# Weights split ahead and kept in DRAM, skewed bias rows, and shifted steps in one branch of a hybrid attention block

## The chip, the cores and the metric

The kernel runs on one core of one Trainium2 chip. The metric is the device time of one execution in microseconds (us), the median of several runs. The core has five engines that run in parallel, each through its own queue in order: TensorE (PE, with its weight loads as PEld), VectorE (DVE), ScalarE (ACT), GpSimd (POOL) and SyncE (SP). SP issues all DMA transfers here.

## The reference

One layer of a streaming encoder on 1024 tokens of width 1024, in float32. Two token mixers run beside each other: branch A is softmax attention over a band of 9 chunks of 64 tokens with a learned bias by clipped distance, branch B is stick-breaking attention, causal, without softmax. Each has 8 heads of 64 channels. Both are projected, gated by a sigmoid of two further projections of x, added, projected again, and a layer norm and a gated feed-forward part of width 2816 with a second layer norm follow.

```
h = x @ w_in[l]
qa, ka, va, qb, kb, vb, ga, gb = jnp.split(h, split_pts, axis=-1)
y_a = chunk_band_attention(heads_a(qa), heads_a(ka), heads_a(va), rel_bias[l]) @ w_proj_a[l]
y_b = stick_breaking_attention(heads_b(qb), heads_b(kb), heads_b(vb)) @ w_proj_b[l]
gate_a = jax.nn.sigmoid(ga + b_gate[l, :D])
gate_b = jax.nn.sigmoid(gb + b_gate[l, D:])
mix = (gate_a * y_a + gate_b * y_b) @ w_out[l]
x = layer_norm(DEEPNORM_ALPHA * x + mix, ln1_g[l], ln1_b[l])
g, u = jnp.split(x @ w_ffn_in[l], 2, axis=-1)
x = layer_norm(DEEPNORM_ALPHA * x + (jax.nn.silu(g) * u) @ w_ffn_out[l], ln2_g[l], ln2_b[l])
```

In branch A the bias of a query i and a key at position p of its band is `rel_bias[h, clip(512 + i - p, -256, 256) + 256]`, so the bias row of each query is that of the one before, moved by one place.

## The kernel before

**Numbers.** TensorE multiplies in a fast type with fewer bits, so each float32 operand is split into a high part (an ACT copy into that type) and a low part (a subtract of the high part, on DVE or POOL), and each product is three matmuls: high by high, high by low, low by high. `split` (line 108) and `begin_w` (line 430) do this. A weight tile is 128 x 1024.

**Stages.** (1) The start, and stage one to about 343 us: q, k, v of both branches and the first five pairs of gates, as 17 pairs of weight tiles. One pair is seven products of twelve matmuls over sums and differences of operands, run by `run_pairs` (line 410) over the steps of `pair_steps` (line 182). Each product ends in a PSUM bank which ACT copies or DVE adds out, and which a later product of the same pair goes on to fill. `left` and `right` load and split the weights of the next pairs while one runs, `also` is called after each pair, and q, k, v and the gates are stored to DRAM. (2) Attention, 343 to 661 us, described below. (3) Branch B's projection to 705 us, the output projection and first layer norm to 797 us, and the feed-forward part to the end.

**The order of attention** is written out by hand in the loop at line 821. It runs over 16 heads (8 of A, then 8 of B), each with 12 value steps: 8 for the first half of the queries (g 0) and 4 for the second (g 1). At a step the loop
- loads q, k and the bias of a head two ahead (`load_qk`, at step 8) and v of the next head (`load_v`, at step 4);
- issues score blocks up to the number in `LEAD` (line 37): eight of 128 queries for each head. `LEAD[0]` is A's, `LEAD[1]` B's; its entry at a step says how many blocks, counted from the head's first, have been issued by then, and more than 8 means blocks of the next head. A's block (`soft_block`) is a score product of two matmuls for each of one or two cuts into a bank `sc`, a DVE reduction that adds the bias and finds the extreme, an exponential on ACT, a reciprocal on DVE and a scaling on POOL. B's block (`stick_block`) has two sigmoids on ACT, a running product on DVE and a product on POOL;
- counts down the list `later` of delayed jobs and runs those that are due;
- transposes a block of the weights (`turn`: TensorE into `tp`, then a split by ACT and DVE into `pt`);
- issues filler matmuls (`fill_until`) and, once more than `LAG` = 2 are pending, the oldest value product (`mult`) into the single bank `pv`. The last product of a half is followed by an ACT copy of that bank into `yt` or `yv`, a small transfer and, three steps later, a POOL add.

**The fillers** (`fill_all`, line 695) are TensorE work that depends on no head: the remaining six gate products (`gate`, gates 10 to 15) and, when A's heads are done, A's projection (`yAps`). For each, `begin_gate` or `begin_proj` loads the weight's tile raw from the inputs, and half a product later ACT makes the high part and POOL the low one.

**The bias of a head** (`rel_bias_tile`, line 556). `small_inputs` (line 315) writes one row of 896 values for each head to DRAM, reversed by DVE. For a head, a transfer whose rows start one element apart brings 128 x 640 values to `braw`, ACT reverses and negates them into `bias`, and POOL sets two corners.

**`split_y`** (line 765) splits a finished output of two heads for the projections; for the last tiles it is put on `later`, two steps after the POOL add.

**Memory.** `SLOTS` names groups of 128 x 1024 tiles in SBUF; QKV is a ring of eight of them that stage one uses for its results. A tile's next use waits until its last use is done, whichever queue that is on.

Of the kernel before, what the change touches and what calls it, by code (L numbers as in the profile page):

```python
# [33 lines left out]


LAG = 2
LEAD = ((6, 7, 9, 9, 10, 10, 11, 11, 12, 12, 13, 13), (7, 8, 9, 9, 10, 10, 11, 11, 12, 12, 13, 14))

FILL = (18.0, 42.0)

# [7 lines left out]
def hybrid_trunk_kernel(ctx: ExitStack, tc, x, xt, w_in, b_gate, rel_bias, w_proj,  # L48
# [29 lines left out]
    def dram(name, n):  # L78
        return [dr.tile([P, 1024], F32, name=f"{name}{i}") for i in range(n)]
# [24 lines left out]
    ORDER = (1, 2, 6, 5, 7, 3, 4)  # L104
    s_dr = [[dram(f"s_dr{g}_{hf}_", 7) for hf in range(2)] for g in range(4)]
    rel_dr = dr.tile([8, 896], F32, name="rel_dr")

    def split(dst_h, dst_l, src):
        nc.scalar.copy(dst_h, src)  # L109
# [205 lines left out]
    def small_inputs():  # L315

        rel_sb = cycle(QKV, "rel_sb")[0:8, 0:896]
        rel_in = cycle(QKV, "rel_in")[0:8, 0:N_REL]
        dma(rel_in, rel_bias)
        nc.vector.tensor_copy(rel_sb[:, 383:896], rel_in[:, ::-1])  # L320
        nc.vector.tensor_copy(rel_sb[:, 0:383], rel_in[:, 512:513].to_broadcast([8, 383]))
        dma(rel_dr, rel_sb)
        dma(bg, b_gate)

    def store_hl(d, hi, lo):
# [30 lines left out]
    def project(i):  # L356
# [50 lines left out]

        return pair_steps(f"p{i}", Wa[i], ops_x, c, done, "pv" if i == 3 else "mm")

    def run_pairs(steps, left, right, also=lambda i: None, first=2, aside=lambda i: None,  # L410
                  then=lambda: None):

        n = len(steps)
        for j in range(first):
            steps[j][0]()
            steps[j][1]()
        then()
        for i in range(n):
            rest = steps[i][2:] if i < first else steps[i]
            for j, p in enumerate(rest):  # L420
                p()
                if j == 0 and i + 1 < n:
                    right(i + 1)
                if j == 1 and i + 2 < n:
                    left(i + 2)
                aside(i)
            also(i)
# [16 lines left out]
    def load_w(*args):  # L444
        return begin_w(*args)()

    def of(tag):
        return lambda name, dtype=F32: slot(tag, name, dtype)

    def begin_gate(i, lo_eng):  # L450
        return begin_w(w_in[24 + (i % 2) * 8 + i // 2], f"g{i}", of("op"), of("op"), lo_eng)

    def gate(i, w, half_way, freed=None):
# [49 lines left out]
    def rest_of_start():  # L503
# [3 lines left out]
        for kt in range(4):  # L507
# [2 lines left out]

    run_pairs([project(i) for i in range(1, len(work))],
              lambda i: left(i + 1) if i > 2 else left_again(3) if i == 2 else None,
              lambda i: right(i + 1), first=3, then=rest_of_start, also=lambda i: small_inputs() if i == 2 else None)
    first_gate = 2 * N_GATE
    first_w = begin_gate(first_gate, nc.vector)()


# [36 lines left out]
        return [t[0][:, 0:512], t[0][:, 512:896], t[1][:, 0:256], t[1][:, 256:384]]  # L554

    def rel_bias_tile(head):
        braw = slot("kp", f"braw{head}")
        src = rel_dr[head:head + 1, 0:640]
        dma(braw[:, 0:640],
            bass.AP(tensor=src.tensor, offset=src.offset, ap=[[1, P], [1, 640]]))  # L560
        bias = slot("kp", f"bias{head}")
        nc.scalar.activation(bias[:, 0:640], braw[:, 0:640][:, ::-1], AF.Copy, scale=-1.0)  # L562
        nc.gpsimd.memset(bias[0:DH, 576:640], BIG)  # L563
        nc.gpsimd.memset(bias[DH:P, 0:DH], BIG)
        return bias
# [66 lines left out]
    def value_steps(hd, g, wt):  # L632

        br, h = hd["br"], hd["h"]
        reach = (4, 8)[br]
        q0 = 4 * g
        nm = f"{'ab'[br]}{hd['n']}_{g}"
        pv = []

        kbs = [4, 5, 6, 7, 3, 2, 1, 0] if g == 0 else [7, 6, 5, 4]  # L640
        steps = []
        for i, kb in enumerate(kbs):
            lo_q = max(q0, kb - reach)
            hi_q = min(q0 + 3, kb)
            n = (hi_q - lo_q + 1) * P
            pts = []

            def turn(kb=kb, lo_q=lo_q, hi_q=hi_q, n=n, pts=pts):
                tp = bank("tr", f"tp_{nm}_{kb}")
                for qb in range(lo_q, hi_q + 1):  # L650
                    tr(tp[:, (qb - lo_q) * P:(qb - lo_q + 1) * P],  # L651
                       wt[qb - q0][:, (kb - qb) * P:(kb - qb + 1) * P], ident)
                pt = slot("pt", f"pt_{nm}_{kb}", F32R)
                split(pt[:, 0:n], pt[:, HW:HW + n], tp[:, 0:n])
                pts.append(pt)

            def mult(i=i, kb=kb, lo_q=lo_q, n=n, pts=pts):
                v = hd["v"]
                if i == 0:
                    pv.append(bank("pv", f"pv_{nm}"))  # L660
                last = i == len(kbs) - 1
                cs = slice((lo_q - q0) * P, (lo_q - q0) * P + n)
                pt = pts[0]
                mm(pv[0][:, cs], v[:, kb, :], pt[:, 0:n], start=(i == 0), stop=False)
                mm(pv[0][:, cs], v[:, kb, :], pt[:, HW:HW + n], start=False, stop=last)
                if last:
                    yt = hd["yt"]()
                    r = slice(h * DH, (h + 1) * DH)
                    gs = slice(g * HW, (g + 1) * HW)
                    if hd["i"] == 7:  # L670
                        nc.scalar.copy(yt[r, gs], pv[0][DH:P])
                        nc.vector.tensor_tensor(yt[r, gs], pv[0][0:DH], yt[r, gs], ALU.add)
                    else:

                        if g == 0:
                            hd["yv"] = slot("yt", f"yv_{nm}")
                        yv = hd["yv"]
                        both, other = (yt, yv) if h == 0 else (yv, yt)
                        nc.scalar.copy(both[:, gs], pv[0])
                        dma(other[r, gs], both[(DH, 0)[h]:(P, DH)[h], gs])  # L680

                        def add():
                            nc.gpsimd.tensor_tensor(yt[r, gs], yt[r, gs], yv[r, gs], ALU.add)
                            if h == 1 and g == 1:
                                if hd["i"] > 4:
                                    later.append([2, lambda: split_y(hd["i"], yt, nc.gpsimd)])
                                else:
                                    dma(y_dr[hd["i"]], yt)
                        later.append([3, add])

            steps.append((turn, mult))
        return steps


    def fill_all():
        w = first_w
        got = []
        for i in range(first_gate, 15):
            end = begin_gate(i + 1, nc.gpsimd)
            yield from gate(i, w, lambda: got.append(end()))  # L700
            w = got.pop()
        end = begin_proj(0, 0, "op", nc.gpsimd)
        ends = {}

        def freed(k):
            if k == 0:
                got.append(end())
            if k < 4:
                ends[k] = begin_y(k, nc.gpsimd)
            if k > 1:  # L710
                ends.pop(k - 2)()

        yield from gate(15, w, lambda: None, freed)
        w = got.pop()
        gates = {0: begin_gA(0)}
        for cc in range(4):
            if cc < 3:
                end = begin_proj(0, cc + 1, "op", nc.gpsimd)
            for j in range(2):
                c = 2 * cc + j  # L720
                t = gates.pop(c)
                squash(t, c, 0)
                if c < 7:
                    gates[c + 1] = begin_gA(c + 1)
                for hf, cs in enumerate((LO, HI)):
                    acc = bank("mm", f"yAps{c}_{hf}")
                    if j == 1 and hf == 0 and cc < 3:
                        got.append(end())
                    for k in range(4):
                        ks = slice(j * HW + k * P, j * HW + (k + 1) * P)  # L730
                        for n, (lw, rx) in enumerate(((w[0], yh), (w[0], yl), (w[1], yh))):
                            mm(acc, lw[:, ks], rx[k][:, cs], start=(k == n == 0),  # L732
                               stop=(k == 3 and n == 2))
                            yield 1.0
                    nc.vector.tensor_tensor(t[:, cs], acc, t[:, cs], ALU.mult)
                if c < KEEP:
                    dma(m_dr[c], t)
                else:
                    kept[c] = t
                if c == 0:  # L740
                    end_y = begin_y(4, nc.gpsimd)
                elif c == 1:
                    end_y()
            if cc < 3:
                w = got.pop()
# [75 lines left out]
    for si, (hd, g, st, box) in enumerate(vsteps):  # L821
# [18 lines left out]
        goal += FILL[hd["br"]] / nhead  # L840
        fill_until(0.5 * (last + goal))
        pend.append(mult)
        if len(pend) > LAG:
            pend.pop(0)()
        fill_until(goal)
    for m_ in pend:
# [391 lines left out]
```

## Time and profile before

| | us |
|---|---|
| median of 3 runs | 1454.58 |
| lowest and highest | 1454.35, 1455.19 |
| the profiled execution's own time | 1453.11 |
| its span in the trace | 1451.1 |

The granted TensorE clock was 0.998 of full speed. Where the trace is read below, rows give an engine, a line of the kernel, the operation, the tile written, an arrow and the tiles read, with a count or a time. `[0.54 <-DVE st_a L582]` says that the engine had been idle for 0.54 us, and that what ended the wait was DVE's instruction of that line. Rows of the table by stage give the stretch and its length, then busy time and instructions of PE, PEld, DVE, ACT and POOL, the granted clock, the share of the DMA engines and GB/s. Ends of matmuls are modelled, so a busy PE may still be waiting. Transfers are told by issue on SP's queue; in the list of transfers the last two figures are KB of one and us from issue to landing. One stall is counted once in each queue that shows it (PE and PEld), so the two are not added.

### The profile page before, as it was taken

The page shows a single profiled execution, that of the slowest core. Times are in us where ns is not written, and L with a number is a line of the kernel's source. Part 1 is how long each engine was busy: PE and PEld are TensorE (multiplying, and loading weights), DVE is VectorE, ACT ScalarE, POOL GpSimd, SP SyncE. Part 2 cuts the span into 40 slices and gives each one's busy share as a digit, 9 for nine tenths or more (in the row PEclk, how much of TensorE's full clock was granted, in tenths as well). Part 3 has the DMA queues.
Part 4 walks back from the last instruction along what each step waited for, and adds up shares of the span by engine and source line. Part 5 has one row for each costly group of instructions (what it writes and reads, how often), then busy time and mean ns, then how long its engine had stood idle before and what let it go on. Part 6 is the DMA issues. An engine that isn't in the chain of part 4 may idle for free.

```text
span 1451.1 us, 19140 instructions
## 1 busy us (share of the span) xinstructions
PE 1429.5 (99%) x6748; PEld 1181.2 (81%) x6748; DVE 1024.4 (71%) x1644; ACT 682.7 (47%) x1187; POOL 278.9 (19%) x326
## 2 busy tenths in 40 slices
PE   9999999999999999999999999999999999999997
PEld 7888888888888788877888888888888887888886
DVE  8875565434776878877849966676677755978767
ACT  6444444446878878874313633444444433221201
POOL 0000000003655879850014000000000000100016
PEclk9999999999999999999999999999999999999999
DMA  7555545338667477647502123344444457787602
GB/s 247 156 178 174 174 148 186 110 101 255 196 191 199 131 226 229 204 178 239 186 25 94 66 102 114 134 159 160 160 159 145 151 197 250 286 307 242 205 15 102
DMA packets 83167, 246.15 MB, mean 170 GB/s; under 512 B 10480, under 2 KB 10480, under 8 KB 83072
## 3 DMA queue, kind: packets, MB, share of 16 engines
q1 hardware_dynamic: 83072, 244.94, 50.8%
q8 instruction: 53, 0.87, 0.2%
q14 instruction: 42, 0.34, 0.1%
HBM read 161.51 MB, written 79.72 MB: 166 GB/s over the span
## 4 chain that ended last, share of the span: by engine, by line
PE 90%; DVE 4%; ACT 2%; issue 1%; DMA 1%; POOL 1%; SPq 0%; POOLq 0%; DVEq 0%; ACTq 0%
PE sxf L179 15%; PE sxp L179 12%; PE szf L179 7%; PE dx L1171 6%; PE szp L179 6%; PE syf L179 4%; PE gps L460 4%; PE syp L179 3%; PE dz L1171 3%; PE yAps L732 2%; PE tp_b L651 2%; PE ops L119 2%; PE ops L117 2%; PE ops L116 2%; PE fpswh_h L116 2%; PE fpswh_h L119 2%
## 5 line engine op out<-in xcount | busy, mean ns | idle before, releaser
L1127 POOL TENSOR_TENSOR wdyt<-wdyt 128x512 f32<-128x512 f32 x8 | 10.7, 1336 | 515.7 <-DVE wdgt L1126 485.1
L628 POOL TENSOR_TENSOR w_b<-w_b,kp_b 128x511 f32<-128x511 f32 (+3 forms) x96 | 97.4, 1029 | 26.9 <-DVE kp_b L623 16.9
L623 DVE TENSOR_TENSOR_SCAN kp_b<-kp_b,ident_ps 128x512 f32<-128x512 f32 (+2 forms) x64 | 56.5, 883 | 24.9 <-ACT kp_b L620 24.6
L891 POOL TENSOR_TENSOR mv<-mv,neghalf 128x1 f32<-128x1 f32 x16 | 23.9, 1491 | 210.9 <-DVE mv L890 210.9
L563 POOL MEMSET bias<- 64x64 f32 x8 | 1.2, 145 | 327.8 <-ACT bias L562 327.8
L192 DVE TENSOR_TENSOR c<-sxp,c 128x512 f32<-128x512 f32 x16 | 11.1, 691 | 69.8 <-issue 40.2
L620 ACT ACTIVATE kp_b<-sc_b 128x512 f32<-128x512 f32 (+3 forms) x96 | 48.4, 504 | 23.9 <-PE sc_b L546 22.9
L110 DVE TENSOR_TENSOR pt_b<-tp_b,pt_b 128x512 fp32r<-128x512 f32 (+1 forms) x96 | 50.3, 543 | 8.4 <-ACT pt_b L109 7.7
L179 PE MATMUL szf<-x1S63h,wcf 128*128 128x512 f32 x168 | 55.1, 389 | 0.0
L1102 DVE TENSOR_TENSOR x<-dx,x 128x512 f32<-128x512 f32 x64 | 43.2, 686 | 15.5 <-PE dx L1171 15.5
L110 DVE TENSOR_TENSOR sl<-h,sl 128x512 fp32r<-128x512 f32 x56 | 38.4, 685 | 19.4 <-ACT sl L109 19.4
L593 POOL TENSOR_SCALAR w_a<-w_a,st_a 128x640 f32<-128x640 f32 (+2 forms) x64 | 42.8, 671 | 48.2 <-DVE st_a L592 33.0
L110 DVE TENSOR_TENSOR pt_a<-tp_a,pt_a 128x512 fp32r<-128x512 f32 (+1 forms) x96 | 45.8, 486 | 8.1 <-ACT pt_a L109 6.9
L651 PE MATMUL tp_b<-ident,w_b 128*128 128x128 f32 x288 | 47.7, 274 | 3.7 <-DVE pt_b L110 3.4
L109 ACT CAST pt_b<-tp_b 128x512 fp32r<-128x512 f32 (+1 forms) x96 | 47.3, 499 | 8.2 <-PE tp_b L651 7.4
L109 ACT CAST sl<-h 128x512 fp32r<-128x512 f32 x56 | 34.7, 620 | 33.7 <-PE syf L179 17.1
L116 PE MATMUL ops<-wh_o,mh 128*128 128x512 f32 x128 | 50.2, 392 | 0.0
L119 PE MATMUL ops<-wh_o,ml 128*128 128x512 f32 x128 | 50.0, 391 | 0.0
L117 PE MATMUL ops<-wl_o,mh 128*128 128x512 f32 x128 | 49.9, 390 | 0.0
L621 ACT ACTIVATE w_b<-sc_b 128x511 f32<-128x511 f32 (+3 forms) x96 | 48.5, 506 | 0.0
L109 ACT CAST pt_a<-tp_a 128x512 fp32r<-128x512 f32 (+1 forms) x96 | 40.0, 426 | 18.2 <-PE tp_a L651 16.9
L588 ACT ACTIVATE w_a<-w_a,st_a 128x640 f32<-128x640 f32 (+2 forms) x64 | 44.7, 698 | 5.2 <-DVE st_a L582 4.3
(1890 smaller groups left out, 4807.2 us busy)
## 6 DMA issues: line engine op xcount, KB each, us to landing
s_dr<-sl SPq DMA_DIRECT2D x112, 256.0 KB, 2.3
sd<-s_dr SPq DMA_DIRECT2D x56, 512.0 KB, 4.5
wLf<-in_w_ffn_in_dram SPq DMA_DIRECT2D x22, 512.0 KB, 4.5
wRf<-in_w_ffn_in_dram SPq DMA_DIRECT2D x22, 512.0 KB, 3.6
wRp<-in_w_in_dram SPq DMA_DIRECT2D x17, 512.0 KB, 4.7
wLp<-in_w_in_dram SPq DMA_DIRECT2D x17, 512.0 KB, 5.4
v_dr<-v SPq DMA_DIRECT2D x16, 512.0 KB, 4.5
kl<-k_dr SPq DMA_DIRECT2D x32, 256.0 KB, 5.4
```

Of the source, the lines that this page charges most:

```text
L109: nc.scalar.copy(dst_h, src)
L110: nc.vector.tensor_tensor(dst_l, src, dst_h.bitcast(F32), ALU.subtract)
L116: mm(acc, lh, rh, start=(i == 0), stop=False)
L117: mm(acc, lh, rl, start=False, stop=False)
L119: mm(acc, ll, rh, start=False, stop=(i == n))
L179: mm(acc, lw[:, ks], rx, start=(first and kt == i == 0), stop=(kt == 3 and i == 2), skip_group_check=not first)
L460: mm(acc[hf], lw[:, ks], rx[k][:, (LO, HI)[hf]], start=(k == j == 0), stop=(k == KT - 1 and j == 2))
L621: nc.scalar.activation(be[:, m0:e], sc[:, m0 - c0:n], AF.Sigmoid)
L623: nc.vector.tensor_tensor_scan(kp[:, 0:e], kp[:, 0:e], ident_ps()[:, 0:e], 0.0, ALU.mult, ALU.add)
L628: nc.gpsimd.tensor_tensor(be[:, m0:e], be[:, m0:e], kp[:, m0 - 1:e - 1], ALU.mult)
L651: tr(tp[:, (qb - lo_q) * P:(qb - lo_q + 1) * P], wt[qb - q0][:, (kb - qb) * P:(kb - qb + 1) * P], ident)
L1171: mm(acc, a, b, start=(first and i == n == 0), stop=(i == n - 1 == 1), skip_group_check=not first)
```

## The change

1. **Weights split in stage one.** Nine weights that the fillers use (gates 11 to 15 and the four tiles of A's projection) are loaded after the pairs 7 to 15 of stage one's loop, split there (high part on ACT, low part on DVE) and stored as two tiles in DRAM. In attention `begin_split` loads the two tiles, and no ACT copy or POOL subtract is left for them.
2. **Bias by one transfer.** `small_inputs` negates on ACT and does not reverse; eight transfers inside DRAM write each head's row 128 times, each one element further right. A head's bias is then one transfer, without ACT.
3. **Steps of branch A.** `LEAD[0][1]` is 8 instead of 7, so A's last score block goes out at step 1 instead of step 2, and at step 2 of the second half of A's queries one value product less is taken out, so its first product comes a step later.
4. **`split_y`** of the last tiles is put six steps after the POOL add instead of two.

```diff
-LEAD = ((6, 7, 9, 9, 10, 10, 11, 11, 12, 12, 13, 13), ...
+LEAD = ((6, 8, 9, 9, 10, 10, 11, 11, 12, 12, 13, 13), ...
...
+    skew_dr = [dr.tile([P + 1, 1024], F32, name=f"skew_dr{h}") for h in range(8)]
...
-        nc.vector.tensor_copy(rel_sb[:, 383:896], rel_in[:, ::-1])
-        nc.vector.tensor_copy(rel_sb[:, 0:383], rel_in[:, 512:513].to_broadcast([8, 383]))
+        nc.scalar.activation(rel_sb[:, 0:513], rel_in, AF.Copy, scale=-1.0)
+        nc.scalar.activation(rel_sb[:, 513:896], rel_in[:, 512:513].to_broadcast([8, 383]),
+                             AF.Copy, scale=-1.0)
         dma(rel_dr, rel_sb)
+        for h in range(8):
+            src, dst = rel_dr[h:h + 1, 128:896], skew_dr[h][0:1, 128:896]
+            dma(bass.AP(tensor=dst.tensor, offset=dst.offset, ap=[[1025, P], [1, 768]]),
+                bass.AP(tensor=src.tensor, offset=src.offset, ap=[[0, P], [1, 768]]))
...
+    first_gate = 2 * N_GATE
+
+    def aside_work(i):
+        if i == 2:
+            small_inputs()
+        first = len(work) - 1 - len(ws_dr)
+        if i >= first:
+            store_split(i - first)
...
+    ws_dr = [dram(f"ws_dr{i}_", 2) for i in range(15 - 2 * N_GATE + 4)]
+
+    def store_split(i):
+        n = 15 - 2 * N_GATE
+        if i < n:
+            j = 2 * N_GATE + 1 + i
+            srcs = w_in[24 + (j % 2) * 8 + j // 2]
+        else:
+            srcs = [(cs, w_proj[2 * (i - n) + j][:, 0:HW]) for j, cs in enumerate((LO, HI))]
+        take = lambda name, dtype=F32: cycle(QKV, name, dtype)
+        for d, t in zip(ws_dr[i], load_w(srcs, f"pre{i}", take, take, nc.vector)):
+            dma(d, t.bitcast(F32))
+
+    def begin_split(i, name):
+        hl = [slot("op", f"w{p}_{name}", F32R) for p in "hl"]
+        for d, t in zip(ws_dr[i], hl):
+            dma(t.bitcast(F32), d)
+        return lambda: hl
...
     def begin_gate(i, lo_eng):
+        if i > first_gate:
+            return begin_split(i - first_gate - 1, f"g{i}")
         return begin_w(w_in[24 + (i % 2) * 8 + i // 2], f"g{i}", of("op"), of("op"), lo_eng)
...
-              lambda i: right(i + 1), first=3, then=rest_of_start, also=lambda i: small_inputs() if i == 2 else None)
-    first_gate = 2 * N_GATE
+              lambda i: right(i + 1), first=3, then=rest_of_start, also=aside_work)
...
     def rel_bias_tile(head):
-        braw = slot("kp", f"braw{head}")
-        src = rel_dr[head:head + 1, 0:640]
-        dma(braw[:, 0:640],
-            bass.AP(tensor=src.tensor, offset=src.offset, ap=[[1, P], [1, 640]]))
         bias = slot("kp", f"bias{head}")
-        nc.scalar.activation(bias[:, 0:640], braw[:, 0:640][:, ::-1], AF.Copy, scale=-1.0)
+        dma(bias[:, 0:640], skew_dr[head][0:P, 256:896])
...
-                                    later.append([2, lambda: split_y(hd["i"], yt, nc.gpsimd)])
+                                    later.append([6, lambda: split_y(hd["i"], yt, nc.gpsimd)])
...
-        end = begin_proj(0, 0, "op", nc.gpsimd)
+        end = begin_split(15 - first_gate, "y0_0")
...
-                end = begin_proj(0, cc + 1, "op", nc.gpsimd)
+                end = begin_split(16 - first_gate + cc, f"y0_{cc + 1}")
...
-        if len(pend) > LAG:
+        wait = hd["br"] == 0 and (g, st) == (1, LAG)
+        while len(pend) > LAG + wait:
             pend.pop(0)()
```

More of the change, by code (lines that the diff above doesn't have):

```diff
@@ L36 @@
 LAG = 2
-LEAD = ((6, 7, 9, 9, 10, 10, 11, 11, 12, 12, 13, 13), (7, 8, 9, 9, 10, 10, 11, 11, 12, 12, 13, 14))
+LEAD = ((6, 8, 9, 9, 10, 10, 11, 11, 12, 12, 13, 13), (7, 8, 9, 9, 10, 10, 11, 11, 12, 12, 13, 14))
 FILL = (18.0, 42.0)
```

## The prediction

> **What bounds the kernel now.** I read the page first, then a table of the engines' busy time by stage, then the lists of waits of TensorE's two queues, then the order of time around the longest waits.
>
> ```profile
> span 1451.1 us, 19140 instructions
> PE 1429.5 (99%) x6748; PEld 1181.2 (81%) x6748; DVE 1024.4 (71%) x1644; ACT 682.7 (47%) x1187; POOL 278.9 (19%) x326
> PE 90%; DVE 4%; ACT 2%; issue 1%; DMA 1%; POOL 1%; SPq 0%; POOLq 0%; DVEq 0%; ACTq 0%
> ```
>
> TensorE is busy for 99% of the span and carries 90% of the chain that ended last. The change adds and removes no matmul, so it can only win TensorE's gaps or make new ones. The table by stage (PE, PEld, DVE, ACT, POOL busy) says where the gaps are:
>
> ```profile
> 36.00:343.00 307.00, 306.87 (x1382) 252.99 (x1382) 174.63 (x235) 136.82 (x191) 2.99 (x5) 1.00 0.51 160
> 343.00:366.00 23.00, 22.48 (x130) 18.04 (x129) 17.35 (x70) 20.35 (x47) 11.78 (x18) 1.00 0.74 218
> 366.00:462.00 96.00, 92.76 (x576) 80.83 (x575) 73.49 (x266) 75.56 (x194) 54.90 (x75) 1.00 0.67 197
> 462.00:493.00 31.00, 29.21 (x160) 22.76 (x158) 25.12 (x44) 29.10 (x65) 24.21 (x37) 1.00 0.60 182
> 575.00:635.00 60.00, 56.47 (x310) 46.89 (x309) 49.33 (x70) 46.89 (x102) 48.78 (x62) 1.00 0.63 195
> ```
>
> Stage one (the projections, 36 to 343) leaves 307.00 - 306.87 = 0.13 us: nothing to win there, only to lose. The four stretches of attention leave 0.52, 3.24, 1.79 and 3.53 us, 9.1 in all. What PE and its weight queue PEld waited for (total us, times, longest), PE's two rows first:
>
> ```profile
> PE tp_b L651 <- DVE pt_b L110: 3.4, 5, 1.0
> PE sc_a L545 <- DVE st_a L582: 2.0, 6, 0.5
> ...
> PEld sc_a L545 <- DVE st_a L582: 4.7, 11, 0.7
> PEld pv_a L664 <- ACT yt L679: 2.5, 5, 0.8
> PEld tp_a L651 <- DVE pt_a L110: 1.8, 3, 1.0
> PEld tp_a L651 <- POOL w_a L593: 1.7, 5, 0.7
> PEld pv_a L664 <- ACT yv_a L679: 1.4, 3, 0.5
> ```
>
> The two queues differ because the ends of matmuls are modelled. One head boundary of branch A, in order of time, shows which is nearer, with a later undisturbed pair of transposes:
>
> ```profile
> 398.53 0.38 PE L651 MATMUL tp_a<-ident,w_a 128*128 128x128 f32 x2
> 398.61 0.56 ACT L679 COPY yt<-pv_a 128x512 f32<-128x512 f32 x1
> 399.19 0.40 ACT L588 ACTIVATE w_a<-w_a,st_a 128x128 f32<-128x128 f32 x1
> 399.21 0.19 PEld L545 LDWEIGHTS sc_a<-kh,qs 128*128 128x128 f32 x1 [0.54 <-DVE st_a L582]
> 399.84 0.40 PE L664 MATMUL pv_a<-pt_a,v 128*128 128x512 f32 x1
> ...
> 409.14 0.38 PE L651 MATMUL tp_a<-ident,w_a 128*128 128x128 f32 x2
> 409.28 0.47 PE L460 MATMUL gps<-xh,wh_g 128*128 128x512 f32 x1
> 409.90 0.19 PEld L664 LDWEIGHTS pv_a<-pt_a,v 128*128 128x128 f32 x1 [0.46 <-ACT yv_a L679]
> ```
>
> Two transposes and the next start are 409.28 - 409.14 = 0.14 us apart undisturbed, and 399.21 - 398.53 = 0.68 at the boundary: 0.54 lost, as PEld says. So I size steady stalls by PEld, as an upper bound, and take PE's rows as the lower.
>
> **The change, part by part.** The sum is made against the profiled execution: 1451.1 of span and 2.0 around it are 1453.1 us, 1.5 below the median of the three runs, 1454.58. I carry the difference over to that median.
>
> *Work taken from ACT and POOL in attention.* The rows of the removed operations:
>
> ```profile
> L439 ACT CAST wh_g<-wr_g x6: 1047/1048/1063, 328.2 to 447.1; 128x1024 fp32r<-128x1024 f32 x6
> L440 POOL TENSOR_TENSOR wl_g<-wr_g,wh_g x5: 2374/2404/2406, 337.8 to 470.2; 128x1024 fp32r<-128x1024 f32 x5
> L562 ACT ACTIVATE bias<-braw x8: 722/740/767, 320.9 to 415.9; 128x640 f32<-128x640 f32 x8
> L440 DVE TENSOR_TENSOR wl_g<-wr_g,wh_g x1: 1224/1224/1224, 329.4 to 329.4; 128x1024 fp32r<-128x1024 f32 x1
> ```
>
> Nine weights lose 9 x 1.05 = 9.4 us of ACT and 9 x 2.40 = 21.6 of POOL, and eight bias rows lose 8 x 0.74 = 5.9 of ACT. In their place SP loads two tiles of 512 KB for each weight instead of one; the second transfer comes where 1.05 + 2.40 us of splitting were, so the weight is ready no later. Busy time off the path is worth nothing; what counts is the wait behind which such an operation stands. At the start of branch A (343 to 366) ACT and POOL each ran one behind the other, and the first transposes waited 1.7 us (PEld) for POOL's normalised rows. One cast less ahead of the first exponentials starts them about 1 us earlier. I take 0.8 us won; bounds 0 and 1.7.
>
> *LEAD 7 to 8.* The last score block of each A head (128 wide) now goes out one step earlier, beside the block before it; with its two matmuls go DVE's reduction, ACT's exponential and POOL's scaling of that block, and no transfer. So DVE has read both score banks sooner when the next head's 320-wide halves want them. That removes the cause of sc_a <- st_a. It does not all come back. ACT's order becomes: the three last exponentials, the fifth pt cast, then the yt copy that frees the only pv bank. In the rows above the copy (398.61) stood ahead of the last exponential (399.19); behind it and the cast it would end near 400.05, and the first value product would start at about 400.07 instead of 399.84, 0.23 later. Of 0.54 at a boundary I leave about 0.3: 0.24 won, six times, 1.5 us. Bounds: 4.7 won (the whole PEld row), or 8 x 0.23 = 1.8 lost with no stall gone.
>
> *The extra lag.* At step (g 1, st 2) of branch A the first value product waits one step more, so the single pv bank's copy gets about one transpose and one gate matmul more: 0.07 by the pair above and 0.23 by stage one's steps (twelve matmuls of 512 columns in 2.72 us, below), 0.30 us against the 0.46 shown. Only two matmuls move, and nothing of SP's or POOL's. By the rows of yt and yv_a, 2.5 + 1.4 = 3.9 us over 8 waits; some of these are the boundary's first product. I take 2.2 won; bounds 0.7 (the share that PE's own gaps show, 0.15 in this instance) and 3.9.
>
> *A to B (462 to 493).* POOL no longer has the 2.4 us subtract ahead of the first stick-breaking products, but DVE's scans set most of the 1.8 us there. I take 0.5 won; bounds 0 and 1.8.
>
> *split_y six steps later, and no proj split in branch B.* In order of time, the two places where branch B lost most:
>
> ```profile
> 580.79 1.05 ACT L768 CAST yh<-yt 128x1024 fp32r<-128x1024 f32 x1 [0.49 <-POOL yt L683]
> 585.66 2.39 POOL L769 TENSOR_TENSOR yl<-yraw,yh 128x1024 fp32r<-128x1024 f32 x1
> 586.73 0.63 PE L651 MATMUL tp_b<-ident,w_b 128*128 128x128 f32 x4 [1.02 <-DVE pt_b L110]
> ...
> 627.05 1.05 ACT L768 CAST yh<-yt 128x1024 fp32r<-128x1024 f32 x1 [3.04 <-POOL yt L683]
> 628.17 2.40 POOL L769 TENSOR_TENSOR yl<-yt,yh 128x1024 fp32r<-128x1024 f32 x1 [1.00 <-ACT yh L768]
> 629.89 0.19 PEld L545 LDWEIGHTS sc_b<-kh,qs 128*128 128x128 f32 x1 [0.68 <-ACT w_b L621]
> 631.57 0.44 PE L651 MATMUL tp_b<-ident,w_b 128*128 128x128 f32 x2 [1.00 <-DVE pt_b L110]
> ```
>
> ACT stood 3.04 us in order behind a cast whose input POOL had not finished; queued behind it were the sigmoids of the next block, and behind those DVE's scan, POOL's product and the transposes. With the cast further back both should pass. I take 2.0 us of 1.02 + 0.68 + 1.00 = 2.7; bounds 0 (the cast and the 2.4 us subtract meet another crowded step) and 2.7.
>
> *What stage one pays.* Nine casts (1.05) go to ACT and nine subtracts (1.22) to DVE, one pair of them per pair of products, 19 us: on DVE 174.63 of 307 was busy, on ACT 136.82. SP gets 9 weights more to load and 18 stores. What such a cast stands in front of is a copy that frees a bank:
>
> ```profile
> 316.02 0.59 ACT L209 COPY c<-szp 128x512 f32<-128x512 f32 x1 [2.13 <-PE szp L179]
> L205 ACT COPY c<-sxp 128x512 f32<-128x512 f32 x16 | 9.4, 589 | 32.2 <-PE sxp L179 23.8 <-DMA q_dr<-c 4.6 <-DMA wLp<-in_w_in_dram 3.9
> DMA to landing us min/median/max: 4.1/5.1/5.9
> ```
>
> The last cast goes ahead of the copy at 316.02, where ACT idled 2.13 us: 1.08 us are left over. Copies come one step of twelve matmuls apart, 2.13 + 0.59 = 2.72 us; TensorE needs the bank one such step after the copy could begin, and the copy takes 0.59, so the cast may be another 2.1 us late, about 3.2 in all. The second row is the evidence that a late DMA in ACT's order is survived: 8.5 us of waits for DMAs, while PE lost 0.13. The third row is the landing of the gate weights: a spread of 1.8 us, inside 3.2. I take 0.7 us lost in all. Bounds: 0, and where the spread meets only the 1.08 us, 9 x (1.8 - 1.08) = 6.5 lost.
>
> [...]
>
> *The skewed bias rows.* Eight transfers inside DRAM, 128 rows of 3 KB each, are issued after the store of the relative bias, where SP's next issue was late anyway:
>
> ```profile
> 98.40 0.94 SPq L130 DMA_DIRECT2D wLp<-in_w_in_dram  x1
> 107.89 0.45 SPq L328 DMA_DIRECT2D k_dr<-hi  x1
> ...
> ln1g<-in_ln_g_dram SPq DMA_DIRECT2D x1, 512.0 KB, 4.9
> ```
>
> Eight issues at the 0.45 to 0.94 us of these rows are 3.6 to 7.5 us of the 9.5 us between them. The only transfer that also reads one DRAM row for all partitions landed in 4.9 us. That idle stretch is the cover; without it the weight of the next pair would come some 3 us later. I take 0, bounds 0 and 3. Two ACT copies in place of two DVE copies of 8 partitions: 0.
>
> Sum: -0.8 - 1.5 - 2.2 - 0.5 - 2.0 + 0.7 = -6.3 us, so 1453.1 - 6.3 = 1446.8 on the profiled execution's scale and 1448.3 on the median's.
>
> **Rivals.** The bound of this measurement is about 0.2%, 2.9 us: faster is below 1451.7, slower above 1457.5.
>
> 1. *The stall only moves to the pv bank.* ACT sets the pace of the boundary: the copies of yt fall 0.23 us later eight times (+1.8) and the extra lag wins its lower bound (-0.7); start, transition and B keep their middle, -3.3, and stage one +0.7. Together -1.5: 1453.1. For it: ACT was busy 75.56 of 96 us and its order is the thing changed. Against: ACT loses two casts and some four bias rows of that, about 5 us, so it runs ahead more often.
> 2. *Slower: ACT waits in order for raw weights in stage one.* Place: the nine new casts, ahead of the copies of sz and sx. Price: each microsecond of landing past the 3.2 us that the cast may be late stops TensorE for as much. It decides from the gains and the bound, 7.0 + 2.9 = 9.9 us, 1.1 us for each cast. If SP reaches the raw load later because it waits in its own queue for a slot's earlier store, 1.5 us per cast are 13.5 us: 1454.6 - 7.0 + 13.5 = 1461. In a mild form, the upper bound of 6.5 us worked out above, it ends at 1454.6 - 7.0 + 6.5 = 1454.1. For it: SP is one queue for all transfers and gains 44 issues. Against: the 8.5 us of such waits survived already.
> 3. *All the stalls go.* The upper bounds of the gains, 1.7 + 4.7 + 3.9 + 1.8 + 2.7 = 14.8 us, with nothing lost: 1439.8. Against: DVE was busy 73.49 of 96 us in branch A and is not relieved at all; a stall removed shows the next one.
>
> **How the numbers follow.** Forecast 0.50, rival 1 0.18, rival 2 0.06 in its mild form and 0.17 in its strong one, rival 3 0.09. The forecast's own range, from the terms' bounds taken half way, is 1444 to 1452. To hold 8 in 10 it takes in rival 1 and most of rival 2: 1443 to 1460. Faster by over 0.2%: nearly all of the forecast (0.47), rival 3 and a little of rival 1, together 0.61. Within 0.2%: most of rival 1, the mild form of rival 2 and the rest of the forecast, 0.21. Slower: the strong form and a remainder, 0.18.
>
> **What would show it right or wrong.** Stage one's row should keep PE within 1 us of its length; a PE wait on sxp or szp behind ACT, with a DMA named as what ACT waited for, is rival 2. In branch A the row sc_a <- DVE st_a should fall to half of 4.7 and pv_a <- ACT by more than half of 3.9; if the second grows instead, it is rival 1. In branch B the waits of 1 us at the casts of yh should be gone, with ACT's 3.04 us idle gone. After 661 us nothing should differ but the start time. The prediction is wrong if attention does not shorten by at least 3 us, or if stage one lengthens by more than 3.

## The result, and the profile after

The changed kernel took 1456.86 us (median of 19 runs, 1453.96 to 1461.32) against 1454.27 for the kernel before (19 runs, 1452.93 to 1456.33): a ratio of 1.0016, 95% interval 1.001 to 1.0023. It is slower by 2.6 us in the medians, where 6.3 us of gain were forecast. The granted clock differs from run to run: the four runs with a mean of 0.999 took 1453.96 to 1456.22 us, the six with 0.996 or less 1457.25 to 1461.32. Its profiled execution took 1456.86 us, with a span of 1455.1; that is 4.0 us above the span of the profile before, more than the medians differ.

The stage table of the profile after, with the columns as before:

```profile
36.00:343.00 307.00, 306.54 (x1381) 252.70 (x1380) 183.01 (x242) 141.99 (x198) 0.87 (x6) 1.00 0.66 214
343.00:366.00 23.00, 22.26 (x133) 18.18 (x132) 17.51 (x71) 18.10 (x44) 9.31 (x16) 1.00 0.77 234
366.00:462.00 96.00, 93.14 (x575) 80.34 (x575) 72.22 (x264) 70.53 (x188) 48.95 (x70) 1.00 0.76 226
462.00:493.00 31.00, 28.92 (x160) 23.44 (x159) 25.85 (x44) 26.27 (x63) 22.79 (x36) 1.00 0.69 200
575.00:635.00 60.00, 55.58 (x294) 45.45 (x292) 46.58 (x65) 43.35 (x96) 40.21 (x54) 0.97 0.60 186
```

Stage one carries the nine new splits and is still full: 306.54 of 307.00, 0.33 us less than before. ACT and POOL did lose the work in attention (in the third row 70.53 for 75.56 and 48.95 for 54.90), and TensorE gained only 0.4 us of it. In the last row it lost 0.9 more, and the granted clock, the figure after the busy times, is 0.97: TensorE did not run at full speed there.

The starts of single products say where the 4.0 us are. The last value product of branch A starts at 482.8 us before and 482.1 after; the first product behind attention (`yBps`, branch B's projection) starts at 660.9 before and 664.3 after. So branch A ends a little earlier, and branch B alone is 4.1 us longer.

The waits of TensorE's two queues, after:

```profile
PE tp_b L682 <- DVE pt_b L111: 3.6, 4, 1.1
PE sc_a L580 <- DVE st_a L613: 0.5, 1, 0.5
...
PEld pv_a L695 <- ACT yt L710: 4.0, 7, 0.8
PEld pv_a L695 <- ACT yv_a L710: 3.5, 6, 0.8
PEld tp_a L682 <- DVE pt_a L111: 2.5, 3, 1.0
PEld sc_a L580 <- DVE st_a L613: 2.1, 7, 0.7
```

In branch A the wait of scores for DVE fell from 4.7 to 2.1 us, and the wait of value products for ACT rose from 3.9 (2.5 + 1.4) to 7.5. In branch B TensorE's wait of the transposes for DVE did not fall: 3.4 before, 3.6 after. The place in branch B where the profile after lost most, in order of time, and the table around it:

```profile
580.21 1.05 ACT L799 CAST yh<-yt 128x1024 fp32r<-128x1024 f32 x1 [2.84 <-POOL yt L714]
...
581.16 0.48 ACT L651 ACTIVATE kp_b<-sc_b 128x384 f32<-128x384 f32 x1
...
583.05 0.19 PEld L580 LDWEIGHTS sc_b<-kh,qs 128*128 128x128 f32 x1 [0.68 <-ACT w_b L652]
...
584.73 0.20 PEld L682 LDWEIGHTS tp_b<-ident,w_b 128*128 128x128 f32 x2 [1.38 <-DVE pt_b L111]
...
630.45 1.05 ACT L799 CAST yh<-yt 128x1024 fp32r<-128x1024 f32 x1 [3.02 <-POOL yt L714]
...
580.00:585.00 5.00, 3.54 (x18) 2.21 (x16) 3.14 (x4) 4.79 (x11) 3.84 (x7) 1.00 0.67 164
585.00:590.00 5.00, 5.00 (x21) 4.13 (x20) 3.24 (x6) 1.32 (x5) 3.09 (x6) 0.66 0.25 90
```

ACT waits 2.84 us in order at the cast of `yh` for POOL's add. That is the pattern seen at 627 us before; now it stands here too, where before ACT had waited 0.49. The wait seen before has not gone: it is the 3.02 us at 630.45. Behind the two gaps TensorE is granted a clock of 0.66 over five microseconds, so 5 x 0.34 = 1.7 us are lost on top.

### The profile page after: what moved, and what is told of

Its sections match the earlier page's. It is cut to its first block, busy times and chain, and to the rows that moved or that the text cites. A ratio compares the mean times of both kernels' runs of the same rounds, so it can differ in the third digit from the quotient of the medians.

```text
span 1455.1 us, 19212 instructions
## 1 busy us (share of the span) xinstructions
PE 1430.6 (98%) x6748; PEld 1181.5 (81%) x6748; DVE 1032.4 (71%) x1651; ACT 675.4 (46%) x1179; POOL 256.9 (18%) x317
## 4 chain that ended last, share of the span: by engine, by line
PE 88%; DVE 4%; ACT 2%; DMA 2%; issue 2%; POOL 1%; SPq 0%; POOLq 0%; DVEq 0%; ACTq 0%
PE sxf L180 15%; PE sxp L180 11%; PE szf L180 7%; PE dx L1203 6%; PE szp L180 5%; PE syf L180 4%; PE gps L496 3%; PE syp L180 3%; PE dz L1203 3%; PE yAps L763 2%; PE tp_b L682 2%; PE ops L120 2%; PE ops L118 2%; PE ops L117 2%; PE fpswh_h L117 2%
```

## The experiments

Each is compared with the kernel before in runs on the same chip (its medians there lay between 1454.32 and 1454.59 us). First each edit alone. **The late split:**

```diff
-                                    later.append([2, lambda: split_y(hd["i"], yt, nc.gpsimd)])
+                                    later.append([6, lambda: split_y(hd["i"], yt, nc.gpsimd)])
```

> The kernel before with only split_y put six steps after the add. Theory one (the moved cast costs): the cast of yh5 stands ahead of the next block's sigmoids in ACT's order, ACT waits about 2.8 us for POOL's add near 577, TensorE loses the same group of 0.6 and 1.2 us there that it lost at 630 already, and the kernel is 1 to 4 us slower; if TensorE's clock halves behind the gap, 1.7 us of that are the clock. Rival (the new transfers cost, the late split is harmless): within 0.7 us of before.

Measured 1457.18 us, ratio 1.0021 (1.001 to 1.0032): 2.7 us slower, the size of the whole loss. Its profile at the same place, in order of time, and the table:

```profile
581.57 1.05 ACT L768 CAST yh<-yt 128x1024 fp32r<-128x1024 f32 x1 [3.51 <-POOL yt L683]
583.44 0.19 PEld L545 LDWEIGHTS sc_b<-kh,qs 128*128 128x128 f32 x1 [1.15 <-ACT w_b L621]
584.41 0.19 PEld L545 LDWEIGHTS sc_b<-kh,qs 128*128 128x128 f32 x1 [0.68 <-ACT w_b L621]
586.09 0.29 PEld L651 LDWEIGHTS tp_b<-ident,w_b 128*128 128x128 f32 x2 [1.38 <-DVE pt_b L110]
...
585.00:590.00 5.00, 4.00 (x15) 3.24 (x15) 4.42 (x8) 2.40 (x7) 4.45 (x11) 0.66 0.01 3
```

The wait, the gaps and the lower clock are all there without any other edit. The clock is not the whole loss: the three runs of this kernel with a mean clock of 0.998 or 0.999 still took 1456.22 to 1457.18 us. The reason is the order of ACT's queue, which is not the order of the source. With two steps the cast of `yh5` (580.79 us before) stood behind the four sigmoids of the next block (577.97 to 579.21); with six, a later place in the source, it stands ahead of them. The cast of `yh6` kept its place. `yh4`'s split moved too: its cast left 582.11, right behind `yh5`'s, for 550.4. What makes the build choose this order no run here shows.

**The nine weights alone** (`ws_dr`, `store_split`, `begin_split` and `aside_work` of the change, without the rest):

> The kernel before with only the nine weights split in stage one and loaded split in attention. Theory one: stage one loses 0.2 to 0.5 us, attention wins about 1 us between branch A and B, so 0 to 1.5 us faster. Rival (the new transfers cost): 2 to 4 us slower, with waits for landings in attention.

Measured 1455.43 us, ratio 1.001 (1.0001 to 1.0019): slower by 0.1 to 2.8 us, against theory one's sign. One new wait in its profile, in order of time:

```profile
542.11 1.05 ACT L797 CAST yh<-yraw 128x1024 fp32r<-128x1024 f32 x1 [0.51 <-DMA yraw<-y_dr]
543.06 0.58 ACT L708 COPY yt<-pv_b 128x512 f32<-128x512 f32 x1
543.69 0.19 PEld L693 LDWEIGHTS pv_b<-pt_b,v 128*128 128x128 f32 x1 [0.97 <-ACT yt L708]
```

Where `wh_y` was cast before, ACT now reaches the next cast sooner, finds its `yraw` not yet landed, and the copy that frees the pv bank waits behind it. This is only a part of what the profile lost. Its last value product of branch A starts at 482.0 us, 0.8 earlier than before, and its first product behind attention at 661.2, 0.3 later; so up to there the weights cost almost nothing. Most of the 3.2 us by which its span is longer (1454.3 against 1451.1) came near 1222 us, far from the edit, where TensorE waited 2.1 us for DVE instead of 1.5 and was then granted half its clock (0.50 from 1225 to 1227, last section).

**The skewed bias rows alone** (`skew_dr`, the two negating copies on ACT, the eight transfers and the new `rel_bias_tile`):

> The kernel before with only the skewed bias rows. Theory one: ACT loses eight operations of 0.74 us that were not on TensorE's path, so within 1 us of before, faster if anything. Rival (the new transfers cost): stage one's weights come late around 100 us and the kernel is 1 to 3 us slower.

Measured 1453.77 us, ratio 0.9997 (0.9986 to 1.0007): no difference, as theory one has it.

**Branch A's steps alone, and each of the two by itself:**

```diff
-LEAD = ((6, 7, 9, ...
+LEAD = ((6, 8, 9, ...
```

```diff
-        if len(pend) > LAG:
+        wait = hd["br"] == 0 and (g, st) == (1, LAG)
+        while len(pend) > LAG + wait:
             pend.pop(0)()
```

> The kernel before with only the two moves of branch A's steps (LEAD 8 and the extra lag). Theory one: the wait at a head's boundary goes from sc_a behind DVE to pv_a behind ACT, 0.55 to about 0.5 us a head, and the kernel stays within 0.7 us. Rival (a real gain hidden by the other edits): 2 to 4 us faster.

> The kernel before with LEAD 8 alone, without the extra lag. Theory one (the stall only moves from sc_a to pv_a at the boundary): within 1 us of before; the wait at the boundary is about 0.5 us for pv_a in place of 0.55 for sc_a, and the 0.3 us at g 1 stays. Rival (LEAD carries the steps' gain): 2 to 3 us faster.

> The kernel before with the extra lag alone. Theory one (the lag takes away the pv_a wait at g 1 and carries the steps' gain): sc_a keeps its 0.55 us a head, pv_a's 0.3 plus 0.1 us at g 1 are gone, 1.5 to 2.8 us faster. Rival (it moves the wait to the next product): within 0.7 us of before.

Both together took 1452.02 us, ratio 0.9983 (0.9975 to 0.9992): faster by 2.5, so the rival held and not theory one. LEAD alone took 1455.39, 1.0009 (1.0 to 1.0018), the lag alone 1452.28, 0.9986 (0.9977 to 0.9994). The waits of the weight queue in the profile of LEAD alone, then of the lag alone:

```profile
PEld pv_a L664 <- ACT yt L679: 4.3, 7, 0.8
PEld pv_a L664 <- ACT yv_a L679: 4.1, 6, 1.0
PEld sc_a L545 <- DVE st_a L582: 1.9, 6, 0.7
```

```profile
PEld sc_a L545 <- DVE st_a L582: 4.7, 11, 0.7
PEld pv_a L664 <- ACT yt L679: 1.0, 3, 0.5
```

LEAD takes 2.8 us from the wait for DVE (4.7 to 1.9) and adds 4.5 to the wait for ACT (3.9 to 8.4). The lag leaves 4.7 as it was and takes the other from 3.9 to 1.0. The lag carried the gain of the steps.

**What is left of it in company.** The changed kernel with `split_y` put back to two steps, branch A's steps with the bias rows, and with the weights:

> The changed kernel with split_y put back to two steps. Theory one (the late split costs 2.7 us, the rest is near nothing): about 0.1 to 0.2% below the changed kernel, 1452.5 to 1454.5 us, and no gap of 0.6 and 1.2 us near 583. Rival (the edits spoil each other in branch A whatever the split does): within 0.7 us of the changed kernel, about 1456.5.

> The kernel before with branch A's steps and the skewed bias rows. Theory one (without ACT's bias rows the pv_a wait at the extra-lag step comes back, 0.25 us and its 0.11 us after-effect a head): the steps' gain of 2.5 us shrinks by about 2, so 1453.0 to 1454.5 us, and the wait for yv_a and yt at g 1 is seen at every head. Rival (the two gains add): 1451.0 to 1452.0 us.

> The kernel before with branch A's steps and the weights split in stage one. Theory one (taking ACT's casts away spoils part of the steps' gain in branch A, as the bias rows do): 1453 to 1454.5 us, with the waits for yv_a and yt at g 1 back at most heads. Rival (the two gains add, the whole loss is the bias rows with the weights): 1451 to 1452.5 us.

Without the late split the changed kernel took 1454.34 us, 0.9999 (0.9991 to 1.0008), so the late split costs 2.5 us there too. Steps with bias took 1452.46, 0.999 (0.9981 to 0.9999), better than expected and only 0.4 above the steps alone. Steps with weights took 1454.63, 1.0004 (0.9995 to 1.0012): the weights take the steps' 2.5 us away. That is on top of the steps alone; on top of steps with bias, as in the changed kernel, they cost 1.9 (1454.34 against 1452.46), with intervals that overlap.

**The cast moved off ACT.** To take away what makes ACT wait, POOL makes the high part of `yh5` and `yh6` behind its own add, in the changed kernel and in the one with branch A's steps:

```diff
-        nc.scalar.copy(yh[i], raw)
+        if i > 4:
+            nc.gpsimd.tensor_copy(yh[i], raw)
+        else:
+            nc.scalar.copy(yh[i], raw)
```

> The changed kernel with the high part of yh5 and yh6 made by POOL, so that ACT never waits for POOL's add. Theory one (ACT waiting in order at that cast makes the gaps of branch B): both groups of 0.6 and 1.2 us are gone, 2.5 to 5 us faster than the changed kernel, 1452 to 1454.5 us. Rival (POOL is the limit there and its longer work takes the gaps' place): within 1 us of the changed kernel, with the transposes waiting for POOL's products.

> The kernel before with branch A's steps and the POOL cast, without the other edits. Theory one: the steps' 2.5 us and one or two groups of 1.7 us in branch B, together 4 to 6 us faster than before, 1448.5 to 1450.5 us. Rival (POOL is the limit): 1452 us, as with the steps alone.

The changed kernel with it took 1450.74 us, 0.9978 (0.9969 to 0.9987), 6.1 below the changed kernel and more than was expected; the steps with it took 1450.17, 0.9971 (0.996 to 0.9983). In the profile of the first, in order of time, with the group of POOL's casts:

```profile
578.56 0.49 ACT L651 ACTIVATE kp_b<-sc_b 128x384 f32<-128x384 f32 x1 [0.98 <-PE sc_b L581]
580.45 1.04 POOL L800 CAST yh<-yt 128x1024 fp32r<-128x1024 f32 x1
...
586.21 0.42 PEld L682 LDWEIGHTS tp_b<-ident,w_b 128*128 128x128 f32 x4 [0.17 <-issue]
...
L800 POOL CAST yh<-yt x2: 1039/1040/1040, 580.5 to 626.6; 128x1024 fp32r<-128x1024 f32 x2
```

ACT goes on with the sigmoids at 578.56, 2.6 us sooner than the 581.16 of the profile after, and the two gaps are gone. POOL's cast costs it 1.04 us, no more than ACT's 1.05.

**A version that beats both.** The steps, the late split and the POOL cast; then the same without LEAD, with the weights, and with the bias rows:

> The kernel before with branch A's steps, the late split and the POOL cast, without the weights and bias edits. Theory one (the late split was only bad because ACT waited at its cast): the yt copy's wait of 1.9 us near 589, which the steps with the POOL cast alone still had, goes too, so 1448 to 1449.7 us, 0.5 to 2 us below steps with POOL cast. Rival (the late split costs by itself): 1451 to 1453 us.

> The lag, the late split and the POOL cast, without LEAD 8. Theory one (LEAD only moves the boundary's wait and costs about 0.8 us alone): 1446.5 to 1447.7 us. Rival (LEAD helps in company with the lag): 1448.5 to 1449.5 us, and the sc_a waits of 0.55 us a head are back without anything saved elsewhere.

> Branch A's steps, the late split, the POOL cast and the weights split in stage one. Theory one (the weights edit is what costs 3 us between the version without the two transfer edits, 1447.7, and the changed kernel with the POOL cast, 1450.7): 1450 to 1451 us, with new waits for pv_a in branch A and for pv_b near 545 behind ACT's cast of a yraw that lands late. Rival (the bias rows cost it): 1447.5 to 1448.5 us.

> Branch A's steps, the late split, the POOL cast and the skewed bias rows. Theory one (the weights cost): 1447.5 to 1448.5 us, with the g 1 waits of 0.25 us back at some heads. Rival (the bias rows cost): 1450 to 1451 us.

| kernel | us | ratio to before (95%) |
|---|---|---|
| steps, late split, POOL cast | 1447.68 | 0.9957 (0.9945 to 0.9969) |
| the same without LEAD | 1449.15 | 0.9962 (0.9949 to 0.9974) |
| the same with the bias rows | 1449.17 | 0.9968 (0.9957 to 0.9979) |
| the same with the weights | 1451.99 | 0.9986 (0.9977 to 0.9994) |

The first is 6.9 us faster than the kernel before. The late split does no harm once ACT does not wait at its cast. LEAD, which alone gained nothing, is worth 1.5 us by the medians here and 0.7 by the ratios. The intervals overlap, and in the two profiles the first product behind attention starts at 656.4 us with it and at 656.5 without, so it is not shown that LEAD helps here either. The weights cost 4.3 us and the bias rows 1.5 by the medians (for the bias rows the intervals overlap), where it was expected that only one of them would. What the weights cost is seen in their profile, in order of time:

```profile
411.63 0.74 ACT L591 ACTIVATE bias<-braw 128x640 f32<-128x640 f32 x1 [0.79 <-DMA braw<-rel_dr]
413.61 0.19 PEld L574 LDWEIGHTS sc_a<-kh,qs 128*128 128x128 f32 x1 [0.98 <-DVE st_a L611]
...
430.09 0.74 ACT L591 ACTIVATE bias<-braw 128x640 f32<-128x640 f32 x1 [0.97 <-DMA braw<-rel_dr]
432.60 0.19 PEld L693 LDWEIGHTS pv_a<-pt_a,v 128*128 128x128 f32 x1 [1.68 <-ACT yt L708]
...
544.84 0.19 PEld L693 LDWEIGHTS pv_b<-pt_b,v 128*128 128x128 f32 x1 [1.15 <-ACT yt L708]
```

Where each weight is two transfers instead of one, a head's `braw` lands later than ACT reaches it, ACT waits in order (0.79 and 0.97 us in these rows), and the exponentials and the pv bank's copy wait behind it. It is late because SP issues it late: the last head's `braw` at 426.47 us, against 403.45 in the version without the weights. At 426.47 it stands right behind the small transfer into `yv_a` (425.95), not behind a weight, so it is SP's order that changed; what changed it is not shown. The new bias rows have no ACT operation that could wait so, which may be why the two edits together (1450.74) cost less than the weights by themselves; those two intervals overlap. What the bias rows cost is spread thin. The waits of the weight queue in the profile of the best version, and in that of the same with the bias rows:

```profile
PEld pv_a L664 <- ACT yt L679: 2.8, 5, 0.8
PEld pv_a L664 <- ACT yv_a L679: 2.6, 4, 0.8
PEld sc_b L545 <- ACT w_b L621: 0.9, 3, 0.4
```

```profile
PEld pv_a L666 <- ACT yt L681: 3.4, 6, 0.8
PEld pv_a L666 <- ACT yv_a L681: 2.9, 5, 0.8
PEld sc_b L551 <- ACT w_b L623: 1.5, 3, 0.9
```

0.9 us more go to the wait for the pv bank, in two more instances, and 0.6 to a wait of scores. Other rows fall (tp_a <- POOL w_a from 1.7 to 0.8), so these rows show where it goes and do not add up to a price. ACT has less to do there, and its copies of the bank still come later; that its operations stand in another order is the likely reason, which no run isolates.

## Why the prediction failed, point by point

**The term that failed** is *split_y six steps later*: "With the cast further back both should pass", 2.0 us won of 2.7. It costs 2.7 us alone and 2.5 in company. The price of the wait was read rightly: with the cast off ACT, on top of the steps, 1.9 us are won by the medians (1452.02 to 1450.17). What was wrong is the premise that a job issued later in the source stands later on its engine. In the built kernel the cast of `yh5` stood further ahead, the cast of `yh6` where it was, and the bound "0" below left no room for a loss. The forecast argued from the source and did not look at the order of ACT's queue in the built kernel.

**Rival 1 was right about LEAD.** 1.5 us were forecast as won, alone it costs 0.8, because the wait for DVE becomes one for ACT, and a little more (4.7 to 1.9 against 3.9 to 8.4). At the boundary that it worked through, the prediction had the delay about right: from the next head's first score product to the value product 1.95 us were expected (398.12 to 400.07), and the profile after has 1.87 (398.33 to 400.20). The weight queue's wait there is 0.76 us for ACT's copy, where it had been 0.54 for DVE; the prediction kept 0.24 us a head of gain all the same.

**The extra lag** was sized well: 2.2 us forecast, 2.3 measured alone.

**Stage one** held: 0.7 us forecast as lost, 0.33 in the table, with all the nine casts in ACT's order. Rival 2, the slower one, was sought in the wrong stage: in the kernels with the weights and the old bias rows it is in attention that a transfer made late holds up ACT, at `braw` (0.79 and 0.97 us) and `yraw` (0.51). I costed the second transfer of a weight for the weight itself ("ready no later") and not for the other loads on SP's queue. That 1456.86 lies within 1443 to 1460 is luck: the upper end was there for waits in stage one that did not come.

**The start and the passage from A to B**, 1.3 us of gain forecast, can't be told apart in the times from what the weights cost: alone these are 1.0 us slower. In the profile of the weights alone something of the kind was won, 0.8 us by the last value product of branch A, and lost again in branch B. In the profile after both rows lose, 22.48 to 22.26 at the start and 29.21 to 28.92 at the passage, and the row tp_a <- DVE pt_a rose from 1.8 to 2.5 us, so the 0.5 us taken for the passage were not won there.

**The skewed rows in stage one** cost nothing, as taken.

**The sum.** It added gains as if they were independent. Alone the edits measure -2.4 (steps), +1.0 (weights), -0.7 (bias) and +2.7 (late split), +0.6 together; in one kernel it is +2.6. Each of the four is known to about 1.3 us or worse, so this difference of 2.0 is not clear by itself. What is clear is that weights and steps do not go together: +1.0 alone, the weights cost 2.6 on top of the steps, and the intervals of those two kernels do not meet (0.9975 to 0.9992 and 0.9995 to 1.0012). The prediction named a sign of its being wrong, an attention that is not shorter by 3 us: from the first score product to the first product behind attention it took 317.9 us before (343.0 to 660.9) and 321.1 after (343.2 to 664.3).

## What to carry to other kernels

Read where an operation stands on its engine in the built program, not where the source issues it: here a delay in the source moved the cast of `yh5` forward, ahead of four sigmoids, and ACT waited 2.84 us at it where it had waited 0.49. What stood behind it on ACT waited too: the sigmoids began at 581.16 us, and at 578.56 without that cast on ACT. It was cheaper to give the cast to the engine that it waits for, for 1.04 us each on POOL, than to move it. When ACT lost the casts of the weights, it reached its next operation sooner, and a load that had been hidden behind that work became the wait (0.51 us for `yraw`, 0.97 for the pv bank behind it).

## What the runs showed of the hardware

The clock granted to TensorE fell to half behind some short stretches of idle time, and not behind others. In the profile after it fell behind 1.46 us of idle time within five (580 to 585, PE 3.54 busy), to a mean of 0.66 over the next five, and in the late split's profile at the same place (PE 3.87 busy, then 0.66). One microsecond of it in the profile after:

```profile
586.00:587.00 1.00, 1.00 (x4) 0.81 (x3) 1.00 (x1) 0.00 (x0) 0.91 (x4) 0.50 0.00 0
```

It fell at a second place too, in the feed-forward part near 1220 us, which no edit touches. There TensorE waits once for DVE's `gt`. Six profiles show that place by the microsecond. In those of the steps alone and of the weights alone TensorE was idle for 2.1 us, and the clock fell to 0.50 behind it; in those of the bias rows alone (0.6 us), the kernel before (1.5), the changed kernel (1.7) and the late split (1.9) it stayed at 1.00. Two rows of the profile of the steps alone:

```profile
1219.00:1220.00 1.00, 0.00 (x0) 0.00 (x0) 1.00 (x2) 0.00 (x0) 0.00 (x0) 1.00 1.05 404
...
1221.00:1222.00 1.00, 1.00 (x3) 0.75 (x3) 0.32 (x1) 0.00 (x0) 0.98 (x1) 0.50 0.88 342
```

In the kernel before, a stretch of gaps like the first did not bring it down:

```profile
630.00:634.00 4.00, 3.00 (x15) 2.23 (x16) 3.89 (x6) 2.97 (x9) 3.76 (x8) 1.00 0.39 132
```

Nor did the second such stretch of the profile after (631 to 636, PE 3.59 of 5 busy).

Where the clock fell at these two places, it cost the same each time: by the clocks of single microseconds 1.70 us in the profile after (0.52, 0.50, 0.50 and 0.78 from 585 to 589), 1.70 in the late split's, 1.71 in those of the steps and of the weights, so 3.4 us at half speed. What went before it were gaps of 0.7 to 1.4 us, in the weight queue's rows of the profile after and of the late split's, or one of 2.1. What decides that one gapped stretch is hit and another not, these runs do not show. The width of the changed kernel's runs, 7.4 us, is no mark of the change: on the chip of the first experiments 29 runs of the kernel before spread from 1451.62 to 1459.61.
